# A hybrid S5/RWKV-7 block: the gated S5 projection beside the last RWKV halves, the modulation product in four column groups, a third context half early

## The chip, the core and the metric

The kernel runs on one core of a Trainium2 chip. The core has TensorE (PE, matrix products into PSUM), VectorE (DVE), ScalarE (ACT), GpSimd (POOL) and the queues that issue DMAs; they run side by side, each takes its instructions in order, and they wait for one another by semaphores. The metric is the device time of one execution in microseconds (us).

## What is computed

One layer over 256 latent tokens (with 256 context tokens as a prefix), model width 2048, in f32. Cut from the reference:

```python
mod = silu(c) @ ada_w + ada_b                  # six groups of 2048: sh1, sc1, g1, sh2, sc2, g2
z = modulate(rms_norm(h, norm1_w), sh1, sc1) @ w_in     # for context and latent tokens
y_s5 = s5_mixer(z[S5 columns])                 # complex diagonal state space, both directions
y_rw = rwkv_mixer(z_rw + (neighbour_mean(z_rw) - z_rw) * rw_mu)   # 16 heads of 64, both directions,
                                               # latent scans start from the context's final state
glu = gelu(y_s5) @ s5_glu_w                    # 1024 -> 4096
s5_out = glu[:, :2048] * sigmoid(glu[:, 2048:])
rw_out = y_rw @ rw_proj                        # 1024 -> 2048
h = x + g1 * ((gates_a * s5_out + gates_b * rw_out) @ w_o)
h = h + g2 * swiglu(modulate(rms_norm(h, norm2_w), sh2, sc2), w13, w2)
out = rms_norm(h, norm_f)
```

A step of the RWKV scan is `s = s*w - (s kk) (kk a)^T + v k^T`; the kernel works on blocks of tokens, for which it inverts small triangular matrices.

## The kernel before

The program plans itself while it is built. `Kernel.drive` holds a model of each engine's time (`Clock`) and chooses at each step between the next piece of dense work and the background generators (`spawn`); the order it finds is then the fixed order of instructions on each engine. What a thing costs on the chip plays no part once the order is written. Every operation passes through one helper and shows line 315 in the profile, so operations are told apart by the names of their tiles.

**Dense work** (`Dense`, line 353) is a list of weight halves of 128x1024 f32: first w_in (134 halves), then the modulation product (192), `glu` (32), `proj` (16), `wo` (32), w13 and w2. A half is loaded by a DMA on SP into a ring of three tiles, split by ACT into `hi` (a copy in fp32r) and by DVE into `lo` (what is left), and multiplied: each 128x128 tile takes three matmuls of 128x256, hi by xh, hi by xl, lo by xh. Each 128 output rows gather in one PSUM tile `psacc`, which an evacuation (`e_glu`, `e_proj`, ...) takes over.

**The modulation product** (groups g1, sh2, sc2: 6144 columns for one vector `sc` = silu(c)) is different ("raw" mode): no splitting, halves of 256 KB through a ring of four tiles. The vector is the stationary operand, one column of it, the weights stream: two f32 matmuls with output 1x256 a half. Sixteen K tiles accumulate one row of 256; then `e_mod` copies the row (`arow`), two transposes (`psmod`) turn it into columns and DVE adds the bias into `ada`. A record of the profile is half of an f32 matmul, so a half has four records.

**The RWKV chain** is cut into eight halves of two head pairs each: 0 to 3 context, 4 to 7 latent. For a half there are fronts (decay and rates: `pslb`, `SC`, `E`, `H`), backs (`pshg` and `psgp`, K and R products, transposes), then for two halves at once an inversion on DVE (`rw_invert`: 31 steps of `lth` and `Nh`, from `Lh` to `t11h`), two sets of 32x32 products (`pswp`, `pswq`) and the chain itself (`rw_chain`: `psxp`, `psup`, `pssp`, `psy1`, `psy2`, step after step). Latent halves end in a post-processing (`rw_post`: `psmp`, `psvp`, `psgp7`). The memory of the halves comes in slots that `rw_room` opens and closes as stages free memory.

**The stages around the change** (`body`, line 2244): beside w_in run the S5 branch and, once "room" is given, fronts and backs of halves 0 to 3. When the last half of w_in is done, inversion 0 begins, and the modulation product fills PE between the steps of halves 0 to 7. When half 7 is inverted and the product is over, the last chain (6/7) runs; after it the memory of the slots is closed, a ring for `glu` and everything later is opened (`d.open(self.n_mod, d.n)`), S5's result is loaded (`load_gl`), and GLU runs beside the posts of halves 6/7. Of GLU's 32 halves, some stand ahead of a change of memory, at which g2 (the second gates), `ma` (the merged halves written so far) and `hres` (the residual) are loaded by ACT; the rest follow it. Then proj, wo, w13, w2 and the final norm.

## Time and profile before

| | us |
|---|---|
| median of three runs | 2268.24 (2266.14 to 2268.9) |
| the profiled execution | 2264.35 |
| its span | 2262.5 |
| startup and first modulation products, to w_in's first matmul | 125.6 |
| w_in | to 786 |
| RWKV halves beside the modulation product | 786 to 1171 |
| last 32x32 products and chain 6/7 | 1171 to 1220 |
| GLU's first to last matmul | 1224.5 to 1342.0 |
| proj, wo, w13, w2, final norm | 1342 to 2262.5 |

The page says in which engine time is spent on the average; a stage that one engine bounds fills that engine's row, one that a chain of dependent steps bounds fills none. So the table by stage is the one to read, cut where a stage begins, with the granted clock of PE (1.00 is 2.4 GHz, 0.50 is 1.2 GHz). A timeline gives each instruction's start, and in brackets how long its engine had stood idle and what released it.

### The profile page before, as it was taken

How to read it: one execution, taken by the hardware profiler on the slowest of the kernel's cores; microseconds unless marked ns; L12 is line 12 of the kernel's file. 1: busy time of each engine (PE TensorE's matmuls, PEld its weight loads, DVE VectorE, ACT ScalarE, POOL GpSimd, SP SyncE). 2: the span in 40 equal slices, each digit the busy share in tenths (PEclk: the TensorE clock that was granted, in tenths of full speed). 3: DMA queues.
4: the chain of work that ended last, by engine and by line, in shares of the span. 5: the costliest groups of instructions: out<-in, count | busy, mean ns of one | idle time of the engine just before them, and what ended most of it. 6: DMA issues, size and time to landing. Idle time of an engine off the chain costs nothing.

```text
span 2262.5 us, 46694 instructions
## 1 busy us (share of the span) xinstructions
PE 2151.0 (95%) x19036; PEld 1888.8 (83%) x19036; DVE 1484.1 (66%) x2899; ACT 1100.7 (49%) x1908; POOL 150.5 (7%) x312
## 2 busy tenths in 40 slices
...
GB/s 370 336 159 196 175 210 180 129 173 216 222 229 149 154 134 138 159 165 152 127 163 53 264 199 185 183 228 229 226 228 228 227 218 183 182 183 185 181 184 131
DMA packets 155014, 431.65 MB, mean 191 GB/s; under 512 B 26256, under 2 KB 39568, under 8 KB 153904
## 3 DMA queue, kind: packets, MB, share of 16 engines
...
## 4 chain that ended last, share of the span: by engine, by line
PE 74%; DVE 8%; issue 7%; ACT 6%; DMA 4%; POOL 0%; ACTq 0%; SPq 0%; DVEq 0%; POOLq 0%
PE psacc L315 63%; PE adacc L315 2%; ACT AQh L315 1%; PE psyp L315 1%; PE psbu L315 1%; DVE lo L315 1%; DVE Nh L315 1%; DMA nk<-d_kvr 1%; DMA ad<-in_adaP_dram 1%; PE psss L315 1%; DVE lth L315 1%; PE pshg L315 1%; PE pskps L315 1%; PE pslb L315 1%; DVE SC L315 1%
## 5 line engine op out<-in xcount | busy, mean ns | idle before, releaser
L315 DVE TENSOR_TENSOR lo<-w,hi 128x1024 fp32r<-128x1024 f32 x478 | 584.7, 1224 | 406.7 <-ACT hi L315 397.0
L315 ACT ACTIVATE hi<-w 128x1024 fp32r<-128x1024 f32 x478 | 505.0, 1058 | 670.2 <-PE psacc L315 570.5
L315 PE MATMUL psacc<-h,hi 128*128 128x258 f32 x2816 | 509.7, 283 | 1.2 <-ACT hi L315 1.2
L315 PEld LDWEIGHTS psacc<-h,hi 128*128 128x128 f32 x2816 | 436.7, 189 | 1.4 <-ACT hi L315 1.4
L315 PE MATMUL psacc<-hl,hi 128*128 128x256 f32 x2144 | 407.1, 284 | 0.0
L315 PE MATMUL psacc<-h,lo 128*128 128x258 f32 x1408 | 399.0, 283 | 0.8 <-DVE lo L315 0.8
L315 PEld LDWEIGHTS psacc<-hl,hi 128*128 128x128 f32 x2144 | 331.5, 191 | 7.0 <-issue 6.9
L315 PE MATMUL psacc<-hl,lo 128*128 128x256 f32 x1072 | 302.4, 282 | 0.0
L315 PEld LDWEIGHTS psacc<-h,lo 128*128 128x128 f32 x1408 | 266.4, 189 | 1.0 <-DVE lo L315 1.0
L315 PE MATMUL psacc<-hid,hi 128*128 128x256 f32 x1408 | 253.5, 283 | 0.0
L315 PEld LDWEIGHTS psacc<-hid,hi 128*128 128x128 f32 x1408 | 219.6, 192 | 0.0
L315 PEld LDWEIGHTS psacc<-hl,lo 128*128 128x128 f32 x1072 | 204.3, 191 | 0.1
L315 PE MATMUL psacc<-w,sc 128*1 128x256 f32 x768 | 189.1, 388 | 14.4 <-DVE ada L315 5.5
L315 PE MATMUL psacc<-hid,lo 128*128 128x256 f32 x704 | 199.2, 283 | 0.0
L315 PE MATMUL psacc<-hc,hi 128*128 128x256 f32 x832 | 172.3, 288 | 0.0
L315 PEld LDWEIGHTS psacc<-w,sc 128*1 128x1 f32 x768 | 56.0, 84 | 116.5 <-DMA w<-in_adaR_dram 24.3
L315 PEld LDWEIGHTS psacc<-hid,lo 128*128 128x128 f32 x704 | 135.2, 192 | 0.0
L315 PEld LDWEIGHTS psacc<-hc,hi 128*128 128x128 f32 x832 | 127.2, 188 | 2.3 <-issue 1.4
L315 PE MATMUL psacc<-hc,lo 128*128 128x256 f32 x416 | 115.6, 278 | 0.0
L315 PE MATMUL psacc<-gl,hi 128*128 128x256 f32 x512 | 97.8, 293 | 13.6 <-ACT hi L315 9.0
L315 PE MATMUL adacc<-ad,sc 128*2 128x512 f32 x192 | 93.4, 643 | 13.3 <-ACT sc L315 7.3
L315 PEld LDWEIGHTS psacc<-gl,hi 128*128 128x128 f32 x512 | 83.7, 200 | 15.2 <-ACT hi L315 9.2
...
## 6 DMA issues: line engine op xcount, KB each, us to landing
w<-in_w_dram SPq DMA_DIRECT2D x264, 512.0 KB, 4.2
w<-in_win_dram SPq DMA_DIRECT2D x134, 512.0 KB, 4.3
w<-in_adaR_dram SPq DMA_DIRECT2D x192, 256.0 KB, 2.9
ad<-in_adaP_dram SPq DMA_DIRECT2D x48, 512.0 KB, 6.5
w<-in_glu_dram SPq DMA_DIRECT2D x32, 512.0 KB, 4.4
w<-in_wo_dram SPq DMA_DIRECT2D x32, 512.0 KB, 3.6
adg<-in_adaG_dram POOLq DMA_DIRECT2D x32, 512.0 KB, 5.6
ad<-in_adaD_dram SPq DMA_DIRECT2D x16, 512.0 KB, 7.6
```

The lines of the kernel that those rows point to most:

```text
L315: return f(*a, **k)
```

## The change

Four things, of one design.

- *Modulation product.* Its weights are laid out anew: a half has four K tiles of one block of 128 columns. `scp` holds each column of `sc` at place 15 of 31 zeros, so that a window of 16 columns puts it in row j. Four f32 matmuls a half (stationary 128x16, streaming 128x128) write to PSUM partitions 32g to 32g+16, g = 0 to 3: four column groups. 64 halves gather 16 rows in each group; then `e_mod` takes four ACT copies, four products with parts of the identity that add the groups up, and one DVE addition of 16 columns, three times in all instead of 24.
- *Third context half early.* The slot of half 2 is opened at "room", ahead of halves 0/1, so the fronts and backs of three halves, and inversion 0 and its 32x32 products, stand beside w_in.
- *GLU on a ring of its own.* `Dense` may hold two sets of rings. When half 5 is done, a ring with two buffers (`ahead=1`) for GLU is opened in freed memory, S5's result loaded, and GLU's halves follow the modulation product as fill beside halves 6 and 7 and their posts; the ring for proj and later is opened when the chains are over. Merged halves all go to memory (`d_ma`) and are loaded again after GLU; the gates' tiles share the four tiles of the modulation ring.
- *Loads of g2, ma and hres* stand after all of GLU. The planner's cost of an fp32r matmul has a floor of 0.12 us, and of the new product 0.47 of a matmul's; its spans change.

```diff
-SPANS = (None,330,100)
+SPANS = (None,280)
...
-    out["adaR"] = aw[:, 2 * D:5 * D].reshape(8, 2, P, 24, 256).transpose(3, 0, 2, 1, 4).reshape(192, P, 512)
+    out["adaR"] = aw[:, 2 * D:5 * D].reshape(4, 4, P, 48, P).transpose(3, 0, 2, 1, 4).reshape(192, P, 512)
...
             if lhs.dtype == F32R:
-                return n / 2400 + 0.002
+
+                return max(n / 2400 + 0.002, 0.12)
...
-    def open(self, first, cap, side=None):
+    def open(self, first, cap, side=None, ahead=2):
+
+        es = ExitStack()
+        if not self.rings:
+            assert not self.fifo and not self.hi
+            self.loaded = self.prepped = first
+        wr = es.enter_context(self.kern.pool("wr", bufs=ahead + 1, side=side))
+        hr = es.enter_context(self.kern.pool("hr", bufs=ahead + 1, side=side))
+        self.rings.append((first, cap, ahead, wr, hr, es))
+
+    def ring(self, i):
+        return next((r for r in self.rings if r[0] <= i < r[1]), None)
...
         if self.raw():
...
+            job, k = tiles[0]
+            if k == 0:
+                self.opened += 1
+                self.accs[job.id] = self.psd.tile([P, P], F32, tag="acc", name=f"psacc{job.id}")
+            acc = self.accs[job.id]
+            self.kern.clk.side = self.kern.clk.part = 0.47
+            for g in range(4):
+                nc.tensor.matmul(acc[32 * g:32 * g + 16], lhsT=job.rhs(k, g), rhs=self.raws[0][:, g * P:(g + 1) * P],
+                                 start=(k == 0), stop=(k == job.k - 1))
...
-        mods = [Job(16, 256, lambda k: self.sc[:, k, 0:1], lambda acc, b=b: self.e_mod(b, acc)) for b in range(24)]
+        part = lambda k, g: self.scp[:, 4 * (k % 4) + g, 15 - k // 4:31 - k // 4]
+        mods = [Job(64, P, part, lambda acc, q=q: self.e_mod(q, acc)) for q in range(3)]
         for h in range(192):
-            halves.append((A["adaR"][h], [(mods[h // 8], 2 * (h % 8) + e) for e in range(2)]))
+            halves.append((A["adaR"][h], [(mods[h // 64], h % 64)]))
...
+    def e_mod(self, q, acc):
+
+        nc = self.nc
+        yield "scalar", acc
+        ar = self.arow[:, q % 2 * P:q % 2 * P + P]
+        gs = [slice(32 * g, 32 * g + 16) for g in range(4)]
+        for g in gs:
+            nc.scalar.activation(ar[g], acc[g], AF.Copy)
+        self.dense.drop()
+        yield "tensor:1", self.arow
+        tp = self.bank([P, 16], f"psmod{q}")
+        for g in gs:
+            nc.tensor.matmul(tp, lhsT=ar, rhs=self.cs("ident")[:, g], start=(g.start == 0), stop=(g.start == 96))
+        f = 32 + 16 * q
+        yield "vector", tp
+        nc.vector.tensor_tensor(self.ada[:, f:f + 16, 0], tp, self.pc("adab", f, f + 16), op=ALU.add)
...
         yield from self.wait("room")
+        opened("s2", (2,))
         opened("sA", (0, 1))
         yield from self.wait("gates")
-        opened("sB", (2, 3), "right")
+        opened("s4", (4,), "right")
+        opened("s3", (3,), "right")
...
         self.drive(self.n_win)
+        d.open_raw(self.yp, self.n_win, self.n_mod)
...
-        self.drive(self.n_mod, early, all=False, span=SPANS[1])
...
-        d.open(self.n_mod, d.n)
+        self.drive(self.n_mod, early, all=False, span=SPANS[1],
+                   stop=lambda: ("half", 5) in self.flags)
+
+        rooms = self.slotx
+        rooms["s5"].close()
+        d.open(self.n_mod, self.n_glu, ahead=1)
         d.top_up()
+        glx = ExitStack()
+        glp = glx.enter_context(self.pool("glp"))
+        self.gates = {}
+        self.spawn(self.load_gl(glp), "gl")
+        self.drive(self.n_glu, early, all=False)
+
+        rooms["s6"].close()
+        rooms["s4"].close()
+        d.open(self.n_glu, d.n, side="right")
+        d.top_up()
...
+        with self.pool("yw", side="right") as yw:
+            late.append(self.spawn(self.load_yr(yw), "yr"))
+            self.drive(self.n_glu, late)
...
+        for k in range(0, 16, 4):
+            nc.scalar.dma_start(self.g2[:, k:k + 4], self.d_gate[1, :, k:k + 4])
+            nc.scalar.dma_start(self.ma[:, k:k + 4], self.d_ma[:, k:k + 4])
+        self.mg = [mgp.tile([P, 16, T], F32R, tag=f"mg{e}", name=f"mg{e}") for e in range(2)]
+        for k in range(0, 16, 4):
+            nc.scalar.dma_start(self.hres[:, k:k + 4], A["xT"][:, k:k + 4])
+        self.drive(self.n_proj, drain=False)
```

How instructions stand now, at three places. First VectorE at the end of w_in, around the beginning of inversion 0 (`Lh`); `lo` is a half of w_in. Before, where the last `lo` of w_in lies further up:

```order
L315 SCALAR_TENSOR_TENSOR SC_4_1_9181<-cst,SC_4_1_9181 128x256
L315 TENSOR_SCALAR AK_4_1_9182<-AK_4_1_9182,hka 128x256
L315 SCALAR_TENSOR_TENSOR AK_4_1_9182<-AK_4_1_9182,kt_4_8962 128x256
L315 TENSOR_TENSOR AK_4_1_9182<-AK_4_1_9182,kt_4_8962 128x256
L315 STREAM_TRANSPOSE Lh_9248<-dch_9192 128x1024
L315 TENSOR_TENSOR lth_0_9285<-Lh_9248,Nh_9249 128x31
L315 TENSOR_TENSOR Nh_9249<-Nh_9249,lth_0_9285 128x31
L315 SCALAR_TENSOR_TENSOR H_4_0_9328<-AK_4_0_9046,SC_4_0_9045 128x4x64
```

and now:

```order
L315 STREAM_TRANSPOSE Lh_8815<-dch_8693 128x1024
L315 TENSOR_TENSOR lth_0_8853<-Lh_8815,Nh_8816 128x31
L315 TENSOR_TENSOR Nh_8816<-Nh_8816,lth_0_8853 128x31
L315 TENSOR_TENSOR AK_5_0_8738<-AK_5_0_8738,kt_5_8656 128x256
L315 TENSOR_TENSOR lth_1_8865<-Lh_8815,Nh_8816 128x60
L315 TENSOR_TENSOR Nh_8816<-Nh_8816,lth_1_8865 128x30x2
L315 TENSOR_TENSOR lo_8872<-w_8683,hi_8856 128x1024
L315 TENSOR_TENSOR lth_2_8894<-Lh_8815,Nh_8816 128x87
```

The inversion moved ahead: thirteen halves of w_in are split (`lo`) between its steps, where none was.

Second TensorE at w_in's last matmuls (`hl` is the normed latent input), before:

```order
L315 MATMUL psacc_0_9214<-hl_178,hi_9139 128x256
L315 MATMUL psacc_0_9214<-hl_179,hi_9139 128x256
L315 MATMUL psacc_0_9214<-hl_178,lo_9161 128x256
L315 MATMUL psvt_4_9335<-cst,v_4_8965 128x128 x2
L315 MATMUL psvt_4_9335<-cst,v_4_9327 128x128 x2
L315 MATMUL pshg_4_0_0_9359<-KR0h_9319,H_4_0_9328 128x64
L315 MATMUL pshg_4_0_1_9360<-KR1h_9320,H_4_0_9328 128x64
```

and now:

```order
L315 MATMUL psacc_0_9520<-hl_179,hi_9479 128x256
L315 MATMUL psacc_0_9520<-hl_180,hi_9479 128x256
L315 MATMUL psacc_0_9520<-hl_179,lo_9491 128x256
L315 MATMUL pswqh_1_9701<-AQh_7898,w1h_9537 32x32 x32
L315 MATMUL pshg_5_1_0_9781<-KR0h_8451,H_5_1_9591 128x64
...
L315 MATMUL psacc_9799<-w_9737,scp 16x128 x4
...
L315 MATMUL psxph_0_9836<-SV0h_7617,KR0h_7612 64x64
L315 MATMUL psxph_0_9836<-SV1h_7618,KR1h_7613 64x64
```

The 32x32 products of inversion 0 (`pswq` the last of them) moved to w_in's end, and chains 0/1 (`psxp`) stand 22 rows behind it, with four halves of the modulation product (`w,scp`) ahead; before, `psxp` came 127 rows behind w_in's end.

Third TensorE inside the last chain (halves 6 and 7, `pssp` to `psy2`), before:

```order
L315 MATMUL pssph_0_13934<-SV0h_11699,HT0h_11697 64x64
L315 MATMUL pssph_0_13934<-SV1h_11700,HT1h_11698 64x64
L315 MATMUL psuph_0_13943<-xsh_0_13910,AQh_13034 64x64 x8
L315 MATMUL psy2h_0_13958<-AQh_11696,SV0h_11699 64x64
L315 MATMUL psy2h_0_13958<-AQh_11696,SV1h_11700 64x64
```

and now:

```order
L315 MATMUL pssph_0_14678<-SV0h_11930,HT0h_11928 64x64
L315 MATMUL pssph_0_14678<-SV1h_11931,HT1h_11929 64x64
L315 MATMUL psacc_0_14589<-gl_13521,hi_14474 128x256
L315 MATMUL psacc_0_14589<-gl_13522,hi_14474 128x256
L315 MATMUL psacc_0_14589<-gl_13521,lo_14477 128x256
...
L315 MATMUL pssph_0_14699<-SV0h_13330,HT0h_13328 64x64
L315 MATMUL pssph_0_14699<-SV1h_13331,HT1h_13329 64x64
```

GLU's matmuls now stand between steps of the chain.

## Rows read from the trace of the kernel before

**Rows 1.** The page, busy time of each engine: us, share of the span, instructions.

```profile
PE 2151.0 (95%) x19036; PEld 1888.8 (83%) x19036; DVE 1484.1 (66%) x2899; ACT 1100.7 (49%) x1908; POOL 150.5 (7%) x312
```

**Rows 2.** Table by stage: stretch, us, busy us (instructions) by engine, PEclk, DMA share, GB/s.

```profile
640.00:786.00 146.00, 143.61 (x1568) 133.54 (x1566) 84.17 (x144) 97.24 (x178) 20.85 (x45) 0.99 0.58 176
786.00:850.70 64.70, 55.56 (x525) 30.63 (x523) 43.17 (x120) 39.27 (x89) 4.71 (x13) 0.79 0.40 123
850.70:888.60 37.90, 34.26 (x523) 22.63 (x523) 23.18 (x58) 31.55 (x79) 10.03 (x21) 1.00 0.42 114
888.60:1005.30 116.70, 105.79 (x1154) 57.80 (x1152) 87.35 (x225) 74.72 (x180) 17.02 (x38) 0.99 0.54 159
1005.30:1138.50 133.20, 123.60 (x1446) 69.72 (x1446) 101.56 (x260) 79.20 (x180) 13.95 (x30) 0.97 0.51 154
1138.50:1171.00 32.50, 22.98 (x102) 7.40 (x100) 26.21 (x70) 3.04 (x5) 0.00 (x0) 0.98 0.59 184
1171.00:1183.60 12.60, 7.75 (x256) 7.34 (x256) 0.00 (x0) 11.13 (x16) 0.00 (x0) 0.50 0.21 49
1183.60:1219.80 36.20, 29.31 (x648) 24.97 (x648) 12.78 (x40) 18.27 (x49) 1.07 (x2) 0.96 0.12 41
1219.80:1342.00 122.20, 103.29 (x784) 100.39 (x785) 68.70 (x94) 60.48 (x90) 11.26 (x21) 0.92 0.66 212
1342.00:2262.00 920.00, 902.77 (x7494) 901.71 (x7493) 553.25 (x791) 394.24 (x478) 17.46 (x33) 0.99 0.65 198
```

**Rows 3.** Timeline of VectorE, an inversion's first and another's last instruction: start, us, instruction.

```profile
786.82 1.24 DVE L315 STREAM_TRANSPOSE Lh<-dch 128x1024 f32<-128x1024 f32 x1
...
1168.97 2.00 DVE L315 STREAM_TRANSPOSE t11h<-Nh 128x1024 f32<-128x1024 f32 x1
```

**Rows 4.** Timeline of TensorE, the sets that move: start us, us, what, count [idle before].

```profile
849.64 1.13 PE L315 MATMUL pslb<-wad,lw 64*128 64x256 f32 x4
...
929.58 1.98 PE L315 MATMUL pswph<-t11h,AQh 32*32 32x32 f32 x64
...
942.25 2.21 PE L315 MATMUL pswqh<-AQh,w1h 32*32 32x32 f32 x128
...
1178.32 3.62 PE L315 MATMUL pswqh<-AQh,w1h 32*32 32x32 f32 x126 [0.30 <-ACT w1h L315]
```

**Rows 5.** Timeline of TensorE, first steps of chains 0/1.

```profile
850.86 0.22 PE L315 MATMUL psxph<-SV0h,KR0h 128*64 128x64 f32 x1
850.87 0.22 PE L315 MATMUL psxph<-SV1h,KR1h 128*64 128x64 f32 x1
```

**Rows 6.** Table by stage of the modulation product's instructions alone (PE, PEld, ACT).

```profile
888.60:1005.30 116.70, 58.71 (x246) 17.57 (x244) 0.00 (x0) 0.99 0.54 159
1005.30:1138.50 133.20, 66.66 (x276) 20.38 (x276) 0.00 (x0) 0.97 0.51 154
```

**Rows 7.** The page, DMA issues: count, KB each, median us to landing.

```profile
w<-in_adaR_dram SPq DMA_DIRECT2D x192, 256.0 KB, 2.9
...
w<-in_glu_dram SPq DMA_DIRECT2D x32, 512.0 KB, 4.4
```

**Rows 8.** The page, costliest groups: busy, mean ns | idle before.

```profile
L315 DVE TENSOR_TENSOR lo<-w,hi 128x1024 fp32r<-128x1024 f32 x478 | 584.7, 1224 | 406.7 <-ACT hi L315 397.0
L315 ACT ACTIVATE hi<-w 128x1024 fp32r<-128x1024 f32 x478 | 505.0, 1058 | 670.2 <-PE psacc L315 570.5
```

**Rows 9.** Table of two later stretches, TensorE alone: the w13 stage.

```profile
1480.30:1992.30 512.00, 510.09 (x4228) 1.00 0.71 216
```

**Rows 10.** Timeline of ScalarE and its DMA issues within GLU.

```profile
1254.34 0.38 ACT L315 ACTIVATE glth<-psacc 128x256 f32<-128x256 f32 x1 [1.54 <-PE psacc L315]
...
1263.50 0.33 ACTq L315 DMA_DIRECT2D ma<-d_ma  x1
...
1268.72 2.95 ACT L315 ACTIVATE hi<-w 128x1024 fp32r<-128x1024 f32 x3
```

**Rows 11.** Timeline of TensorE at the same place.

```profile
1269.83 0.80 PE L315 MATMUL psacc<-gl,hi 128*128 128x256 f32 x2 [9.04 <-ACT hi L315]
```

207 lines of the change are left out of this document (92 added, 115 removed).

## The prediction

> **What bounds the kernel now.** I read the page's busy times first, then a table by stage, then single engines at the seams. TensorE (PE) is busy 95% of the span [rows 1], which hides that the middle is not bound by it. In the table [rows 2] the last stretch (GLU's end to the finish) keeps PE at 902.8 of 920.0 us, and the stretch before 786 at 143.6 of 146: dense matmuls, back to back. Between them lie 556 us of the RWKV chain, cut at the starts of the four inversions and of the chains: 64.7 + 37.9 us (w_in's end to inversion 2), 116.7 and 133.2 (to inversions 4 and 6), then 32.5 + 12.6 + 36.2 + 122.2 = 203.5 to the end of GLU. Here the order of dependent steps is the bound: an inversion holds VectorE (DVE), then 32x32 products, then a chain in which PE, ScalarE (ACT) and DVE take turns. The four inversions follow one another and each period is filled with halves of the modulation product. Two things in the table are to be seen: DVE is busy only 84 of 146 us before 786, while an inversion (786.8 to about 823, and 32.5 us for the last) needs it; and from 1138 to 1342 the tail has three stretches with an idle engine: DVE at 0.0 in 12.6 us, no modulation product in the 36.2 us of the last chain, and PE at 103.3 of 122.2 afterwards, although 768 GLU matmuls wait. [Rows 3] give the first inversion's start and the last one's end.
>
> **The sum, by stages, against the profiled run's own span of 2262.5 us.** Its time was 2264.35, so 1.85 us lie around the span; the median of the three runs is 2268.24, 3.9 above that run. I carry both over.
>
> *1. w_in gets longer, +16 us.* The third context half brings three sets of K/R products, three LoRA sets, two transposes of v, and the two pairs of 32x32 products of inversion 0 into the stretch where PE is full. A LoRA set took 1.13 us, one head pair's pswp 1.98, the two pswq together 2.21, and 3.62 at a granted clock of 0.50 [rows 4, 2]. With 1.2 us for a set of sixteen (estimate from the LoRA set): 3 x 1.2 + 3 x 1.13 + 2 x 0.6 + 2 x 1.98 + (2.21 to 3.62) = 14.4 to 15.8, rounded up for waits. DVE gets the inversion (36 us) and about 13 us of fronts: 84.2 + 49 = 133 of 162 us, full but not over. Should `lo` come late because it stands behind substitution steps, PE waits: +25. Below +8 I see no way, since PE has no gap there. w_in ends at about 802.
>
> *2. w_in's end to inversion 2, −52 us.* Of the 102.6 us the first 64.7 (inversion 0, its products, fronts) now lie before w_in's end. What remains is a set of products, four modulation halves (together about 5 us), the chain of halves 0/1 with what follows it (37.9 us) and some front work of halves 6/7 that stood beside the inversion, 7 us: 50 us. Ends: 45 and 62.
>
> *3. Inversion 2 to inversion 6, −8 us.* Before, the product's records number 246 and 276, four to a half, so 62 + 69 = 131 halves, busy 125 us of PE [rows 6], 0.95 us each. After, 153 halves stand there. Their cost I can bound from both sides. Four matmuls of 128 columns stream as many columns as two of 256, so one after another they cost 0.95 again. If the four column groups run beside each other, it is about a quarter. For overlap speaks [rows 5]: two matmuls with 64-wide outputs in different halves of the partitions start 0.01 us apart. But the weights are then the limit: a half lands in 2.9 us [rows 7] through a ring of four tiles, so 0.73 us per half in a run of many, and inside the inversions runs of 8 to 15 halves stand. 153 x 0.73 = 112 us, against 125; 13 us saved, of which I take 8, since DVE (87.4 and 101.6 us busy) holds part of that time anyway. Removing 24 ACT copies, 48 transposes and 24 DVE additions, for 12 copies, 12 products and 3 additions, helps the same way and is in the 8. Low end: the first period took 101.8 us with 39 halves, so with free halves the two periods could go to 203.6, −46; half of it, −25, is my end. High end: +15, all 153 at 0.95 on the path and no help.
>
> The Trainium skill, "TensorE: Matmul & The Clock Gate", Part 3 ("Measured speedup vs the span model"), gives 2.38 times for three column tiles; that would make an estimate of 0.35 us for a half and, by itself, put stage 3 near its low end. The trace of before has no such matmul with 16-wide outputs to test it.
>
> *4. Inversion 6 to GLU's end, 203.5 to 167, −36 us.* After, 18 modulation halves and 228 of the 768 GLU matmuls stand beside inversion 6, 54 beside the 32x32 products, 60 inside the last chain, 72 among its post-processing, 354 after it. A matmul of this form takes 512.0 / 4228 = 0.121 us [rows 9], so the five parts are 27.6, 6.5, 7.3, 8.7 and 43 us. Inversion: 32.5 us alone, plus some ten `lo` and gate operations on DVE, 42 us (PE: 18 x 0.73 + 27.6 = 41, level with it). Products: 12.6 plus part of the fill, 18. Chain: 36.2 alone with PE 29.3 busy, plus 7.3 of fill of which most finds a gap, plus ACT's `hi` in its queue, 41. Posts: 9 of fill plus steps, 16; they took from 1219.8 to 1249 before, when GLU's first weights and gl arrived only then. The rest: 43 us at full rate, but this ring has two buffers, and a half needs 4.4 us to land [rows 7] plus 1.06 for `hi` and 1.22 for `lo` [rows 8]: 6.7 / 2 = 3.3 us per half against 2.9 of PE, 50 us at worst; 47. Sum 42 + 18 + 41 + 16 + 47 = 164, with 3 for seams 167. Ends: −50 and −15.
>
> *5. A stop at the start of proj, +7 us.* The gates' second half, the merged halves and the residual are now loaded by twelve DMA issues on ACT, behind GLU's last tanh. The same series before: from the tanh at 1254.34 the first `ma` issue came at 1263.50 and the next `hi` at 1268.72 [rows 10], and PE stood 9.04 us [rows 11]. That stop lay inside the 203.5 and is gone there. Now three halves (8.7 us of PE) are ready as cover: 13.8 of ACT plus `hi` 1.06 and `lo` 1.22 less 8.7 is 7. Ends 5 and 16 (a wait for all of GLU's writes). From there 920 us are instruction for instruction as before.
>
> Span: 802 + 50 + 242 + 167 + 7 + 920.5 = 2188.5; the run 2190; the median of runs, with the 3.9, **2194 us**.
>
> **Rivals.** *The column groups don't overlap.* Then 153 halves cost 0.95 each, 145 us instead of 112, and stage 3 comes to +16, stage 4 loses 4: 2222. For it: nothing before writes 16-wide outputs. Against: [rows 5].
>
> *GLU is fed one half at a time.* `hi` and `lo` stand in order behind chain steps that wait for PE, and two buffers leave little slack. At 6.7 us for each of the 22.5 halves behind inversion 6, 151 us stand against 122 in my sum: +29, 2223. Against: before, GLU kept PE at 103.3 of 122.2 us among the same post-processing, with the 9-us stop in it [rows 2, 11]; but there it had three buffers.
>
> *The modulation product becomes cheap*, 0.3 us a half, when the ring refills during chain steps: stage 3 at −40, 2162.
>
> *Slower: TensorE at the lower clock through the chains.* When PE worked little, the granted clock fell: 0.50 in 1171 to 1183.6, 0.79 in 786 to 850.7 [rows 2]; the pswq pair took 3.62 us there instead of 2.21 [rows 4]. The new product gives PE fewer busy microseconds between inversions. A chain has about 28 us of PE work; four chains at 1.2 instead of 2.4 GHz would add 4 x 28 = 112 us and give about 2305. It decides the sign where the mean clock in the chains falls below 0.6: 112 x (1/0.6 − 1) = 75, all of the gain. Against: the last chain, with no dense matmul in it at all, ran at 0.96 [rows 2].
>
> By the Trainium skill, "TensorE: Matmul & The Clock Gate", Part 1 (the clock gate), a PE that has gone idle runs at 1.2 GHz until it has been busy again; this speaks against thinning the fill, and the 0.50 stretch agrees while the 0.96 one shows that chain steps alone can be enough.
>
> **How the numbers follow.** My forecast with its neighbourhood (2170 to 2212) gets 0.60, cheap modulation 0.10, the first two rivals or a mix of them (2212 to 2250) 0.20, the slow clock or a w_in stretched by starving 0.07 slower, 0.03 for the same time. Two runs of this kernel can be told apart from about 0.2%. The terms' ends, added as independent errors (9, 9, 20, 18 and 5 us), make some ±30 us; the upper end goes on to the two smaller-gain rivals: 2165 to 2238. Faster 0.90, same 0.03, slower 0.07.
>
> **What would show it.** Step 1: the last hl matmul at 795 to 810, and DVE over 80% before it. Step 2: psxp of halves 0/1 within 6 us of w_in's end, inversion 2 at about 852. Step 3: four w,scp records starting together and runs of halves at 0.7 to 0.8 us each with PE waiting for their DMA; inversion 6 near 1094. Step 4: gl matmuls between the steps of the last chain, GLU over at about 1261. Step 5: PE idle 5 to 16 us some 9 us into proj, ended by `hi`. Wrong would be: w,scp records in file (first rival), gl waits of 3 us on `hi` after `hi` (second), a clock under 0.7 in the chains (last), or proj to the end longer than 920 us.

## The result: faster by 1.5%, under half of the forecast gain

The changed kernel takes 2233.96 us in the median of 4 runs (2230.21 to 2238.72) against 2268.32 for the kernel before (4 runs beside it): a ratio of 0.9851, 95% interval 0.9831 to 0.9871. The sign held, and the time lies at the upper end of the range of 2165 to 2238; the gain is 34 us where 74 were forecast. That the range held is luck in part: 12.8 us of the gain come from stages that the prediction took to be unchanged, and without them the time would be about 2247. The profiled run of the changed kernel is its slowest of the four, 2238.72 us with a span of 2236.9, so the stages below add up to 25.6 us and not to 34. Runs of one program differ by up to 18 us (2212.4 to 2229.99 in e6 below), and w_in ends between 823.3 and 833.8 us in kernels with the same order up to there, the profile of after being the latest of them. So I read differences of stages below some 5 us from single profiles, and of w_in below some 10, as nothing, unless several kernels show them.

The page after has less work on TensorE (2151.0 us in [rows 1]) and as much on the others:

```profile
PE 2093.1 (94%) x19780; PEld 1889.1 (84%) x19780; DVE 1472.3 (66%) x2879; ACT 1103.1 (49%) x1897; POOL 156.6 (7%) x325
```

Table by stage of the kernel after, same columns as [rows 2] (stretch, us, busy us (instructions) of PE, PEld, DVE, ACT, POOL, granted clock, DMA share, GB/s). Cuts: 126 (end of the start), inversion 0's begin, w_in's end, begin of inversions 2, 4 and 6, end of inversion 6, begin and end of the last chain, GLU's end, proj's end, finish:

```profile
126.00:771.20 645.20, 629.24 (x5484) 607.09 (x5484) 481.43 (x1089) 340.80 (x683) 69.75 (x141) 0.98 0.55 173
771.20:833.80 62.60, 59.24 (x637) 57.33 (x636) 52.50 (x113) 37.77 (x61) 4.42 (x10) 0.96 0.46 142
833.80:896.30 62.50, 51.85 (x899) 37.46 (x900) 32.51 (x81) 48.87 (x124) 11.35 (x26) 0.83 0.52 163
896.30:1004.10 107.80, 85.46 (x1410) 55.49 (x1410) 84.78 (x213) 67.32 (x159) 16.98 (x38) 0.75 0.62 190
1004.10:1154.60 150.50, 118.02 (x1848) 76.28 (x1848) 103.38 (x255) 84.27 (x184) 10.93 (x24) 0.69 0.57 183
1154.60:1190.60 36.00, 32.20 (x250) 28.99 (x250) 33.27 (x80) 11.95 (x20) 4.90 (x9) 0.79 0.50 159
1190.60:1215.80 25.20, 23.48 (x457) 22.09 (x458) 8.59 (x10) 22.25 (x38) 2.15 (x4) 0.93 0.40 128
1215.80:1243.70 27.90, 27.45 (x573) 24.44 (x573) 15.39 (x43) 16.75 (x41) 2.62 (x5) 1.00 0.22 69
1243.70:1314.40 70.70, 62.27 (x465) 58.97 (x466) 41.21 (x58) 37.22 (x53) 9.74 (x19) 0.95 0.53 171
1314.40:1375.20 60.80, 49.76 (x387) 48.85 (x386) 37.37 (x64) 22.71 (x33) 2.15 (x4) 0.89 0.81 286
1375.20:2236.90 861.70, 844.24 (x7111) 843.16 (x7109) 512.56 (x729) 375.19 (x445) 15.94 (x30) 0.99 0.64 200
```

Against the steps of the sum, in us:

| step | before | after | forecast | measured |
|---|---|---|---|---|
| 1 start to w_in's end | 785.7 | 833.8 | +16 | +48 |
| 2 w_in's end to inversion 2 | 102.9 | 62.5 | −52 | −40 |
| 3 inversion 2 to 4, 4 to 6 | 116.7 + 133.3 | 107.8 + 150.6 | −8 | +8 |
| 4 inversion 6 to GLU's end | 203.4 | 159.8 | −36 | −44 |
| 5 proj | 46.1 | 60.8 | +7 | +15 |
| 6 wo, w13, w2, finish | 874.5 | 861.7 | 0 | −13 |

Steps 1 and 3 lost most of the gain, steps 2 and 5 some more; steps 4 and 6 were better than forecast. In the table of after the clock column is new: 0.83, 0.75 and 0.69 from w_in's end to inversion 6, where [rows 2] had 0.79 to 1.00.

### The profile page after: what moved, and what is told of

It reads as the page before. It is cut to its first block, busy times and chain, and to the rows that moved or that the text cites. A ratio compares the mean times of both kernels' runs of the same rounds, so it can differ in the third digit from the quotient of the medians.

```text
span 2236.9 us, 48212 instructions
## 1 busy us (share of the span) xinstructions
PE 2093.1 (94%) x19780; PEld 1889.1 (84%) x19780; DVE 1472.3 (66%) x2879; ACT 1103.1 (49%) x1897; POOL 156.6 (7%) x325
## 4 chain that ended last, share of the span: by engine, by line
PE 68%; DVE 10%; ACT 9%; DMA 9%; issue 3%; POOL 0%; SPq 0%; ACTq 0%; DVEq 0%; POOLq 0%
PE psacc L315 56%; DMA w<-in_adaR_dram 4%; DVE lo L315 3%; PE adacc L315 2%; ACT hi L315 1%; PE psyp L315 1%; PE psbu L315 1%; ACT AQh L315 1%; ACT L315 1%; DMA w<-in_glu_dram 1%; PE psss L315 1%; DMA ad<-in_adaP_dram 1%; DMA nk<-d_kvr 1%; DMA d_win<-win 1%; ACT SV1h L315 1%
## 5 line engine op out<-in xcount | busy, mean ns | idle before, releaser
L315 PE MATMUL psacc<-hl,hi 128*128 128x256 f32 x2144 | 416.5, 288 | 0.0
L315 PEld LDWEIGHTS psacc<-hl,hi 128*128 128x128 f32 x2144 | 336.9, 193 | 7.8 <-issue 7.2
L315 PE MATMUL psacc<-hid,hi 128*128 128x256 f32 x1408 | 239.4, 276 | 0.0
L315 PEld LDWEIGHTS psacc<-hid,hi 128*128 128x128 f32 x1408 | 211.8, 188 | 0.0
L315 PE MATMUL psacc<-hid,lo 128*128 128x256 f32 x704 | 194.3, 276 | 0.0
L315 PE MATMUL psacc<-w,scp 128*16 128x128 f32 x1536 | 96.5, 362 | 53.5 <-DMA w<-in_adaR_dram 52.1
L315 PEld LDWEIGHTS psacc<-w,scp 128*16 128x16 f32 x1536 | 33.3, 107 | 107.9 <-DMA w<-in_adaR_dram 97.4
L315 PE MATMUL psacc<-mg,hi 128*128 128x256 f32 x512 | 90.5, 279 | 0.0
```

Source lines behind the costliest of these rows:

```text
L315: return f(*a, **k)
```

## The experiments

Times are medians of 4 runs (10 for e8, e9 and e11, one for e12), beside the kernel before on the same chip; a stage time is from the one profiled run. "After" is the changed kernel, and "the tail" the stage from inversion 6 to GLU's end.

**One part alone, or one part taken out.** First the new modulation product in the kernel before, without the other parts.

> The kernel before with the new modulation product alone (four column groups, e_mod three times), nothing else of the change. Theory R (the ring of four weight tiles sets the pace, about 1.07 us a half in runs, as PE's 49 us of waits for these weights in the changed kernel say): the product no longer costs PE 0.95 us a half, but inversions are filled at the ring's pace and PE idles at the lower clock; time between 2255 and 2275. Rival M (the new product itself brings the gain the prediction gave it): 2235 to 2250. Rival N (the product in column groups is what hurts periods 4 to 6): over 2280.

```diff
-                nc.tensor.matmul(acc, lhsT=job.rhs(k), rhs=self.raws[0][:, c * job.n:(c + 1) * job.n], start=(k == 0), stop=(k == 15))
+            for g in range(4):
+                nc.tensor.matmul(acc[32 * g:32 * g + 16], lhsT=job.rhs(k, g), rhs=self.raws[0][:, g * P:(g + 1) * P],
+                                 start=(k == 0), stop=(k == job.k - 1))
...
+        mods = [Job(64, P, part, lambda acc, q=q: self.e_mod(q, acc)) for q in range(3)]
```

Measured 2270.61 us, ratio 1.0019 (1.0004 to 1.0035): the product alone brings nothing, as theory R expected. The two periods between inversions 2 and 6 take 125.5 + 132.4 = 257.9 us (before 250), though PE is busy only 98.1 and 99.3 us in them (before 105.8 and 123.6), at a clock of 0.70 and 0.78.

Then the reverse, the changed kernel with the old product:

> The changed kernel with the old modulation product (two matmuls of 256 columns with a stationary of one column, 24 rows turned by transposes). Theory V (the new product saves PE time that the ring of four weight tiles gives back as waits, 49 us of them; e1 showed no gain from it alone): within 8 us of 2234. Rival U (beside GLU's fill the PE time saved counts): 15 to 35 us slower, 2249 to 2269.

```diff
-        mods = [Job(64, P, part, lambda acc, q=q: self.e_mod(q, acc)) for q in range(3)]
+        mods = [Job(16, 256, lambda k: self.sc[:, k, 0:1], lambda acc, b=b: self.e_mod(b, acc)) for b in range(24)]
```

Measured 2258.74 us, 0.9969 (0.9955 to 0.9982): 25 us slower than after, as rival U had it. The periods between inversions 2 and 6 take 107.0 and 148.3 us, in sum 3 less than in after; the difference lies in the tail, 191.9 us instead of 159.8. The table by stage of this product's matmuls alone in that kernel, from inversion 2 to 4, to 6, and to GLU's end (us, busy us and matmuls, clock, DMA share, GB/s), shows why:

```profile
884.80:991.90 107.10, 51.42 (x213) 0.95 0.49 154
991.90:1140.10 148.20, 75.23 (x300) 0.97 0.54 169
1140.10:1332.00 191.90, 38.16 (x160) 0.97 0.52 164
```

40 halves (160 / 4) are left behind inversion 6 and GLU comes after them; with the new product 6 are left (48 matmuls at eight to a half). The next run keeps the new product and takes out GLU's fill:

> The changed kernel in which GLU's matmuls may not start before chain 6/7 and its posts are done; rings, loads and everything else as in the changed kernel. The prediction's term 4 says that GLU beside halves 6 and 7 is worth 36 us: from inversion 6 to GLU's end 190 to 205 us instead of 160, time 2262 to 2280. If the fill slows inversion and chain by what it brings, less than 15 us are lost, under 2249.

```diff
-        self.drive(self.n_glu, early, all=False)
+        self.drive(self.n_mod, early, all=False)
```

2259.86 us, 0.9971 (0.9958 to 0.9983), and a tail of 189.1 us, both just below the ranges expected. So the fast product without GLU's fill, or the fill's ring without the fast product, leaves the tail at about 190; only both give 160. The two gains are one and the same 25 us, which needs both.

The context half:

> The changed kernel, but the slot of context half 2 is announced only when w_in is done, as in the kernel before; inversion 0 still stands beside w_in. Theory A (w_in's extra 48 us are the moved work, pauses of about 3 us in which PE waits for ACT, and the lower clock behind each pause): without the third half w_in ends 8 to 16 us earlier, at 813 to 822 in the profile, and inversion 2 comes later behind w_in by as much or more; time 2230 to 2250. Rival I (inversion 0 on DVE starves `lo` and is what stretches w_in): w_in still ends at 827 or later.

```diff
-                self.flags[("slot", g)] = 0.0
+                if g != 2:
+                    self.flags[("slot", g)] = 0.0
...
         yield from self.wait("gates")
+        self.flags[("slot", 2)] = 0.0
```

2238.16 us, 0.9874 (0.9853 to 0.9895): the third half is worth some 4 us, within the ranges of the runs. It moved 25 us out of w_in's end to inversion 2 (87.6 without it, 62.5 with it), cost w_in 9 to 20 (814.1 against 823.3 to 833.8), and the tail is 23 shorter without it (136.4 and 159.8), with 103 GLU matmuls ahead of inversion 6. All this is as theory A expected; that ACT makes the pauses, this run doesn't test.

The floor in the planner's cost, which sets no instruction but only their order, alone in the kernel before, and taken out of after:

> The kernel before with one line of the planner changed (the cost of an fp32r matmul at least 0.12 us, as in the changed kernel), so only the order of instructions differs. Theory A says nothing hangs on it: within 5 us of 2266. Rival P (the new plan itself, not what is moved, makes part of the loss in w_in): w_in ends 5 us or more behind 785.7 and the time is over 2272.

```diff
-                return n / 2400 + 0.002
+                return max(n / 2400 + 0.002, 0.12)
```

2251.05 us, 0.9936 (0.9921 to 0.9951). Inversion 0 begins at 752.6 us in this kernel, beside w_in, where before it began at 786.82 [rows 3]; w_in ends 16.7 us later and inversion 2 still begins 6.5 us earlier. So neither expectation held: w_in does end later, as rival P had it, and yet the kernel is faster. The order alone gives 0.64%, some 15 us, over two fifths of what the whole change gives.

> The changed kernel with the planner's old cost of an fp32r matmul (no floor of 0.12 us); only the order of instructions changes. Theory F (the floor is what lets the plan put inversion 0 beside w_in; alone it made the kernel before 0.64% faster): inversion 0 begins at w_in's end or later, w_in ends before 815, inversion 2 comes 80 us or more behind it, time 2240 to 2255. Rival G (the third half's early slot does that by itself): the time stays within 6 us of 2234.

```diff
-                return max(n / 2400 + 0.002, 0.12)
+                return n / 2400 + 0.002
```

2233.03 us, 0.9854 (0.984 to 0.9869), the same as after: theory F was right about the order and wrong about the time. Here inversion 0 stays behind w_in (at 801.2 us), and w_in ends at 797.9. The tables from 126 us to w_in's end, of before, of this kernel and of after (columns as above), part step 1 into its pieces:

```profile
126.00:785.70 659.70, 654.89 (x5836) 636.76 (x5834) 498.09 (x1091) 350.51 (x684) 72.08 (x143) 1.00 0.59 182
```

```profile
126.00:797.90 671.90, 664.16 (x5861) 644.91 (x5860) 497.31 (x1096) 354.96 (x696) 69.01 (x136) 1.00 0.54 177
```

```profile
126.00:833.80 707.80, 688.48 (x6119) 664.41 (x6119) 533.92 (x1201) 378.57 (x743) 74.16 (x151) 0.98 0.54 170
```

Read so, the third half costs 12.2 us, and the inversion beside w_in the other 36: PE's idle time goes from 7.7 to 19.3 us, its busy time from 664 to 688. The floor changes the whole order, so this is the price of the plan that has the inversion there, not of the inversion's own steps: of the 19.3 us, 16.0 lie ahead of its first instruction (645.20 less 629.24 in the first row of the table of after), among the fronts and backs that now have to be ready sooner. How much of the busy time is the clock shows e6 (below), which has the same order up to w_in's end and as much idle time, but is busy 10 us less:

```profile
126.00:823.70 697.70, 678.27 (x6104) 656.33 (x6103) 533.59 (x1199) 378.61 (x742) 72.01 (x145) 0.99 0.53 172
```

So of the 36 us some 12 are waits and 10 a lower clock that another run didn't have; the other 14, the moved products and what e6 itself lost by the clock, stay undivided. What the plan saves behind w_in (107.5 to 62.5) covers the 36 us and 9 more, and those are paid back: periods and tail sum to 403.3 us here, with 103 GLU matmuls ahead of inversion 6, and to 418.2 in after.

**What sets the middle.** The first idea was that the weights' ring lets too few transfers fly.

> The changed kernel with three modulation weight tiles in flight instead of four. Theory R: landing 3.4 us and about 0.9 us of use and reissue over three tiles is 1.43 us a half instead of 1.07; of the 192 halves some 110 stand in runs, so +25 to +45 us, 2260 to 2280. Rival T (the DMA engines' throughput is the limit, not the number in flight): no change, within 6 us of the changed kernel's 2234.

```diff
-        while len(self.raws) < self.RAW and self.raw_next < self.raw_to:
+        while len(self.raws) < 3 and self.raw_next < self.raw_to:
```

2222.1 us, 0.9815 (0.979 to 0.984): 12 us faster than after, which neither theory had. As three tiles are no slower than four, the ring's depth is no limit. In inversion 2, 36 halves are issued in 40.2 us with three tiles and 34 in 40.2 with four; all transfers together move 249 and 243 GB/s there. The planner knows the number of tiles, so the order changes too: inversion 2 to 4 takes longer (121.2 us), the tail less (145.1), with no half left behind inversion 6 and some 20 GLU matmuls ahead of it.

> The changed kernel with half of each modulation weight half loaded (128 KB for 256 KB) and the two column groups that lack theirs fed from the loaded part; the order of instructions is the same. The modulation vectors are not the reference's, all else is computed. Theory R and rival T both expect a faster feed: 0.7 to 0.9 us a half instead of 1.07, 2210 to 2225. If the weights' feed is not what holds inversions 2 to 6, the time stays within 6 us of 2234.

```diff
-            self.nc.sync.dma_start(t, self.halves[self.raw_next][0])
+            self.nc.sync.dma_start(t[:, 0:256], src[:, 0:256])
...
-                nc.tensor.matmul(acc[32 * g:32 * g + 16], lhsT=job.rhs(k, g), rhs=self.raws[0][:, g * P:(g + 1) * P],
+                nc.tensor.matmul(acc[32 * g:32 * g + 16], lhsT=job.rhs(k, g), rhs=self.raws[0][:, g % 2 * P:(g % 2 + 1) * P],
```

2217.38 us, 0.9788 (0.9766 to 0.981), within the expected range, though not by the expected pace (35 halves are issued in the 37.5 us of inversion 2's substitution, 1.07 us each). A half lands in 2.2 us instead of 3.4; inversion 4 to 6 takes 140.8 us instead of 150.6, PE's waits for weights there 16.8 instead of 27.7. The bytes do matter, for about 10 of the 17 us that this period lost.

> The changed kernel; each of the 768 modulation matmuls is followed by one with a stationary of zeros on the same weights and the same PSUM rows, which adds nothing to the sum and keeps PE twice as busy in the inversions (0.82 us a half, still under the feed's 1.07). Theory K (part of the loss in inversions and the 32x32 products is the clock, 0.57 to 0.63 there): clock near 1.0 from 896 to 1150 us, 8 to 25 us faster, 2209 to 2226. Rival R alone: the feed is the whole loss, no change or up to 8 us slower.

```diff
+                for z in range(1):
+                    nc.tensor.matmul(acc[32 * g:32 * g + 16], lhsT=self.kern.zz, rhs=rhs, start=False, stop=last and z == 0)
```

2239.43 us, 0.9882 (0.9861 to 0.9903). The granted clock of the two periods (columns as above) comes back to 0.91 and 0.88, and they take 114.4 and 154.4 us, not less than at 0.75 and 0.69, so theory K's gain did not come:

```profile
890.30:1004.70 114.40, 92.71 (x1960) 68.66 (x1952) 84.89 (x212) 67.36 (x159) 16.98 (x38) 0.91 0.58 180
1004.70:1159.10 154.40, 124.17 (x2600) 94.11 (x2600) 103.69 (x256) 84.96 (x184) 11.67 (x24) 0.88 0.58 184
```

That alone doesn't clear the clock: product and zeros hold PE for 108.0 us in the two periods, where the product alone held it for 78.6, so the periods could have grown by 29 us and grew by 10.5. A gain of up to some 19 us could hide there. The trace of e3 says more. From inversion 4 to its chain, the substitution and the steps behind it, the same instructions run at a clock as low as in after:

```profile
995.75:1033.37 37.62, 29.64 (x354) 16.34 (x356) 33.98 (x97) 8.73 (x25) 2.25 (x5) 0.55 0.48 141
1033.37:1058.27 24.90, 24.70 (x540) 18.78 (x540) 9.20 (x19) 21.42 (x41) 2.13 (x4) 0.58 0.40 121
```

These 62.5 us are 72.3 in after (clock 0.58 and 0.54) and 61.1 in before (1.00 and 0.87). So what this stretch lost against before goes with the bytes of the weights and not with the clock. Whether a higher clock would win something beyond that stays open, as PE is busy in 24.70 of the last 24.90 us.

Next, in-order queues. On SP's queue the loads of the S5 result stand among the modulation weights and wait for VectorE.

> The changed kernel with one edit: the eight loads of the S5 result (bvl from d_y) are issued by POOL instead of SP. Theory Q (they wait for VectorE in SP's in-order queue and hold the modulation weights behind them, so PE stands and inversion 6 comes late): inversion 4 to inversion 6 falls from 150.6 to 135 to 142 us, PE's wait for weights in that period from 27.7 to under 20 us, the kernel from 2234 to 2219 to 2228. Rival D (the halves' landing time and the extra steps on VectorE set it, the queue's order doesn't): 147 to 153 us there, the kernel within 2229 to 2239.

```diff
-                nc.sync.dma_start(raws[k].rearrange("p (t c) -> p t c", c=64), src[k])
+                nc.gpsimd.dma_start(raws[k].rearrange("p (t c) -> p t c", c=64), src[k])
```

2231.2 us, 0.9845 (0.9825 to 0.9865); inversion 4 to 6 takes 148.7 us, PE's waits for weights 25.9. The result loads in SP's queue were not it, and this theory fell. GLU's first four weight loads stand in the same queue and were not moved; in after no modulation load is issued from 1102.6 to 1115.4 us, and PE's longest wait for weights, 5.27 us, ends at 1120.57. VectorE, which prepares inversion 6, has no wait from 1108 to 1121 us, so this one doesn't reach it directly. To find the place I cut the period from inversion 4 to 6 at four landmarks: the end of the substitution (`t11h`), the first and the last addition of `pssp` to the chain's state `S`, and the next inversion:

| inversion 4 to 6, us | substitution | to the chain | chain | to inversion 6 |
|---|---|---|---|---|
| before | 34.8 | 26.4 | 35.5 | 36.6 |
| after | 41.9 | 30.3 | 31.2 | 47.1 |
| old product (e9) | 36.7 | 26.8 | 38.6 | 46.3 |
| half the bytes (e3) | 37.6 | 24.9 | 31.2 | 47.1 |

The first column goes with the product and its bytes, the last with neither. In the substitution of inversion 4, the tables of before and after:

```profile
1005.20:1040.00 34.80, 31.42 (x176) 12.58 (x174) 33.13 (x99) 7.40 (x22) 1.17 (x3) 1.00 0.76 231
```

```profile
1004.00:1045.90 41.90, 29.81 (x356) 15.21 (x354) 33.92 (x96) 8.79 (x25) 2.25 (x5) 0.58 0.75 239
```

VectorE's work is nearly the same (33.13 and 33.92 us); 6.3 of the 7 us are waits. In the list of waits of the same stretch in after, PE for the weights and VectorE for PE and ACT (us in total, times, longest):

```profile
PE psacc L315 <- DMA w<-in_adaR_dram: 11.8, 14, 1.7
```

```profile
DVE KR0h L315 <- PE psgp L315: 2.0, 2, 1.8
DVE SC L315 <- ACT SC L315: 1.9, 1, 1.9
DVE ada L315 <- PE psmod L315: 1.9, 1, 1.9
```

In before, PE waited 1.1 us for weights there, and the list has no wait of VectorE. The front's products (`psgp`) stand in PE's queue behind halves whose weights haven't landed; VectorE's front steps wait for them, and the substitution stands behind these on the same engine. The planner takes 0.73 us for a half's transfer. With the rate that the trace shows:

> The changed kernel, with the planner's transfer rate for the modulation weights set to 240 GB/s instead of 360 (the trace shows 243 to 248 in the inversions); only the order changes. Theory S (PE stands in order behind halves that haven't landed, and the front's products and VectorE's substitution behind it): the substitutions of inversions 2 and 4 take 35 to 38 us instead of 40.3 and 41.9, PE's waits for weights between inversions 2 and 6 fall from 43.9 us to under 30, the kernel to 2216 to 2228. Rival (the waits only move, since the same bytes have to land before GLU): substitutions shorter, but more halves after inversion 6, the kernel within 2229 to 2239.

```diff
-            self.dma = max(self.dma, t0) + n / (360e3 if last >= 128 else 180e3)
+            self.dma = max(self.dma, t0) + n / ((240e3 if "adaR" in src.tensor.name else 360e3) if last >= 128 else 180e3)
```

The substitutions of inversions 2 and 4 fall to 30.1 and 36.1 us, from 40.3 and 41.9, as the mechanism has it. But PE's waits for weights between the two inversions and the sixth stay at 41.9 us (43.9), the steps from the substitution to the chain grow to 39.0 and 38.4, and from the chain to inversion 6 to 61.9, with 122 GLU matmuls already in it. 2243.25 us, 0.9902 (0.9881 to 0.9923): 9 us slower than after, outside both expected ranges. The waits move, they don't go.

The next run explains most of the last column of the table.

> The changed kernel, with the split of the S5 result (eight loads, eight steps on ScalarE, eight on VectorE) not begun before inversion 6 has its inputs. Theory G (these steps stand in the two queues ahead of inversion 6's inputs): from the last step of chains 4 and 5 to inversion 6 37 to 40 us instead of 47.1, from inversion 4 to 6 140 to 144 instead of 150.6; inversion 6 to GLU's end grows by as much or more, because GLU can start only after it: 168 to 175, the kernel 2230 to 2245. Rival: the stretch before inversion 6 stays at 45 to 48 us, since the weights of the last halves set it.

```diff
         src = self.d_y.rearrange("(k p) t c -> k p t c", p=P)
         raws = []
+        yield from self.wait(("back", 15, 0), ("back", 15, 1))
```

2225.95 us, 0.9819 (0.98 to 0.9837); from the chain to inversion 6 40.0 us instead of 47.1, inversion 4 to 6 142.1 instead of 150.6, and the tail grows by only 4 us, to 163.9, so that the kernel is faster than either side expected. VectorE's timeline ahead of inversion 6 (`Lh`) in after (start, us, instruction, in brackets the idle time before it and what ended it) shows how the split `gl` held it:

```profile
1145.09 1.82 DVE L315 COPY dch<-AQh 32x512 f32<-32x512 f32 x2
1150.90 1.13 DVE L315 TENSOR_TENSOR gl<-bvl,gl 128x256 fp32r<-128x256 f32 x2 [3.99 <-ACT gl L315]
1152.06 1.11 DVE L315 COPY dch<-AQh 32x512 f32<-32x512 f32 x2
...
1154.65 1.24 DVE L315 STREAM_TRANSPOSE Lh<-dch 128x1024 f32<-128x1024 f32 x1
```

Two of VectorE's four `dch` copies, which the inversion reads, stand behind a `gl`, which waits for the `gl` of ACT, which stands behind ACT's own `dch` copies and `pR`. From the chain's end on, `gl` and the two `lo` add 6.9 us of VectorE work, and VectorE waits another 6.7 us for ACT's `gl`; the waits cost the period as much as the work. The e18 run still has one such wait of 3.68 us, and its last part is still 3.4 us longer than in before.

**The seam at proj.**

> The changed kernel with the twelve loads of g2, ma and hres issued by POOL instead of ACT. Theory Q (ACT, blocked in its queue by these issues until 18 us after GLU's last tanh, is why proj takes 60.8 us instead of 46.1): proj takes 47 to 51 us, time 2221 to 2227. Rival D (the 6 MB have to land before proj can be evacuated, whoever issues them): proj stays at 57 us or more, time within 5 us of 2234.

```diff
-            nc.scalar.dma_start(self.g2[:, k:k + 4], self.d_gate[1, :, k:k + 4])
-            nc.scalar.dma_start(self.ma[:, k:k + 4], self.d_ma[:, k:k + 4])
+            nc.gpsimd.dma_start(self.g2[:, k:k + 4], self.d_gate[1, :, k:k + 4])
+            nc.gpsimd.dma_start(self.ma[:, k:k + 4], self.d_ma[:, k:k + 4])
```

(and `hres` in the same way.) ScalarE's timeline in after shows the loads in its queue ahead of `hi`:

```profile
1315.25 0.33 ACTq L315 DMA_DIRECT2D ma<-d_ma  x1
...
1327.90 0.33 ACTq L315 DMA_DIRECT2D ma<-d_ma  x1
1328.40 4.26 ACTq L315 DMA_DIRECT2D hres<-in_xT_dram  x4
1332.70 2.00 ACT L315 ACTIVATE hi<-w 128x1024 fp32r<-128x1024 f32 x2 [16.65 <-DMA ma<-d_ma]
```

and TensorE's, where the wait of [rows 11] has its successor:

```profile
1333.81 0.80 PE L315 MATMUL psacc<-yr,hi 128*128 128x256 f32 x2 [9.76 <-ACT hi L315]
```

On POOL's queue the list of waits of proj has instead

```profile
PE psacc L315 <- ACT hi L315: 2.7, 1, 2.7
```

and proj takes 54.3 us instead of 60.8: between the 47 to 51 of theory Q and the 57 of rival D. Before, it took 46.1; of the 14.7 us that proj lost, the queue explains 6.5. The other 8 stay with the loads on POOL. All transfers together move 414 GB/s from 1324 to 1334 us in after, and 404 and 413 in two such stretches of e6, so these loads may hold back proj's own weights; no run shows it. The kernel: 2222.67 us (2212.4 to 2229.99), 0.9821 (0.9797 to 0.9846). Proj's 6.5 us are seen in all four kernels with this edit (52.8 to 54.8 us there); the other 5 us of the median are not sure: the interval reaches into after's.

**Together.**

> The changed kernel with the twelve loads for proj issued by POOL (as in e6) and three modulation weight tiles in flight (as in e2). If the two gains add (each about 11 us): 2209 to 2215. If both are the same gain (a different plan of the middle that gives back what the queue took): 2219 to 2226, no better than either.

2219.53 us, 0.9792 (0.9772 to 0.9813): proj 54.8, tail 145.2. That is 3 us under e2 and e6 each, so the two gains hardly add.

> The changed kernel with both the eight result loads and the twelve loads for proj on POOL. By theory Q the period from inversion 4 to 6 is 135 to 142 us and proj about 54 us: 2208 to 2218. By rival D the first edit adds nothing to e6: 2219 to 2226.

2232.42 us, 0.9849 (0.9821 to 0.9877), slower than both ranges: proj 53.8, but inversion 4 to 6 151.8 and the tail 162.2, so with the S5 results on POOL as well nothing is left of e6's gain beyond run-to-run differences.

> The changed kernel with the result loads and the proj loads on POOL and three modulation weight tiles in flight. If all three add: 2200 to 2212, about 0.972 of the kernel before. If they overlap: 2215 to 2225. Proj 54 us in either case; the sign of the comparison with e15 tells whether three tiles in flight are worth anything once the queue is clear.

2226.15 us, 0.9823 (0.9801 to 0.9844): the three don't add. In e14 the edits are those of e2 and e6, in e15 those of e6 and e13, in e16 all three. The best kernel is e14, three modulation tiles in flight and proj's loads on POOL: 2219.53 us against 2233.96 and 2268.3, its interval apart from both, though not from those of e2, e6 and e18. E18's edit together with these was not tried.

**Two checks of side effects.** The change also sets a size of DMA scratch memory, a line left out of the cut diff:

> The kernel before with one allocation made smaller (4096 bytes of scratch for DMA descriptors, as in the changed kernel), so that every SBUF address moves and not one instruction. The stages behind proj took 12.9 us less in the changed kernel with the same instructions: w2 239.4 instead of 253.4, wo 90.4 instead of 92.2. Theory S (where tiles lie in SBUF sets the pitch of these matmuls, 0.113 or 0.120 us): w2 or wo at a pitch other than 0.120, time 3 to 16 us off 2266. Rival O (the pitch hangs on something else): all stages as in the kernel before, within 3 us.

```diff
-    nc = bacc.Bacc("TRN2", target_bir_lowering=False, num_devices=1)
+    nc = bacc.Bacc("TRN2", target_bir_lowering=False, num_devices=1, dynamic_dma_scratch_size=4096)
```

2265.11 us, 0.9997 (0.9984 to 1.0009), all stages as before, w2 included: rival O's side. Whether the late tiles' addresses moved, the trace doesn't show.

> The changed kernel with one unused tile of 64 bytes per partition among the constants (the tile of zeros of e4, without its matmuls): the addresses behind it move, the instructions of PE stay. Theory S (addresses set the pitch of the late stages; w2 took 239.4 us in the changed kernel, 250.6 in e4, 253.4 in the kernel before): w2 about 250 us. Rival O (what moved in e4 was the stream of PE's instructions, 768 more of them): w2 at 239.4.

```diff
+            self.zz = cpool.tile([P, 16], F32, tag="zz", name="zz")
+            nc.gpsimd.memset(self.zz, 0.0)
```

One run, 2237.85 us: w_in ends 6 us earlier than in after and the tail is 7 us shorter, but w2 takes 250.6 us instead of 239.4. The page's row for the same 1408 matmuls of w2 (busy us, mean ns | idle before), in before, after and this kernel:

```profile
L315 PE MATMUL psacc<-hid,hi 128*128 128x256 f32 x1408 | 253.5, 283 | 0.0
```

```profile
L315 PE MATMUL psacc<-hid,hi 128*128 128x256 f32 x1408 | 239.4, 276 | 0.0
```

```profile
L315 PE MATMUL psacc<-hid,hi 128*128 128x256 f32 x1408 | 250.7, 281 | 0.0
```

By the code, the unused tile shifts the tiles allocated behind it by 64 bytes; the matmuls of that stage are the same, and PE has no idle time there in any of the three.

## Why the prediction was right or wrong

**Step 1, +16 forecast, +48 measured: the step that failed most.** I priced what enters w_in as PE work and took PE to stay full beside it ("133 of 162 us, full but not over" for VectorE). The third half costs 12.2 us (e10), near my 8.2 (its K/R products, LoRA sets and transposes). The inversion and its 32x32 products come to 36 with the plan they need, not 8 (26 in e6, whose w_in ends at 823.7): PE stands idle for 19.3 us since 126 us, where it stood 4.8, and its clock falls. Most of the pauses end with tiles of ScalarE, not of VectorE. Three windows of the table of after, and the one behind the last pause (columns as above):

```profile
660.00:680.00 20.00, 19.48 (x210) 17.87 (x206) 11.24 (x25) 18.60 (x33) 3.89 (x8) 1.00 0.42 125
680.00:700.00 20.00, 18.12 (x144) 16.09 (x144) 11.16 (x17) 17.73 (x35) 1.08 (x2) 1.00 0.44 145
700.00:720.00 20.00, 16.78 (x128) 15.08 (x126) 17.10 (x30) 14.49 (x25) 4.48 (x12) 0.89 0.63 201
720.00:740.00 20.00, 20.00 (x130) 17.63 (x129) 10.26 (x21) 12.22 (x27) 2.27 (x7) 0.68 0.34 108
```

Of the waits that the list of after names for PE from 640 to 833.8 us, 8.7 us end with tiles of ACT and 3.3 with tiles of VectorE, 1.4 of these with `lo`:

```profile
PE psvt L315 <- ACT HT0h L315: 2.8, 1, 2.8
PE pswqh L315 <- ACT w1h L315: 1.7, 2, 1.3
...
PE psacc L315 <- DVE lo L315: 1.4, 2, 1.0
```

ACT is busy 18.60 and 17.73 of 20 us in two of the windows. That its load is what makes these tiles late is argued, not shown: in before, ACT was busy 17.70 us from 720 to 740, and PE stood idle for 0.44. Behind a pause the granted clock falls: 0.68 from 720 to 740, with PE busy all of the 20 us. I had named "PE waits: +25" for a late `lo`; 14.5 us of waits came, few of them on `lo`, and the clock I had not put into this step at all.

**Step 2, −52 forecast, −40 measured.** The right mechanism; 12 us are missing. The 8 us behind w_in's end ran at a clock of 0.50 and the rest of the stage at 0.88, which may be where they went; no run tests it. But steps 1 and 2 belong together, and my −36 for both turned out +8. E10, in which the inversion stays behind w_in, ends at the same time: in this plan, pulling it in beside a full w_in wins nothing, since w_in pays 36 us and the rest is paid back behind it. E7 shows that with two context halves instead of three the same overlap pays: w_in +17 us, inversion 2 nevertheless 6.5 earlier.

**Step 3, −8 forecast, +8 measured: two sub-steps failed.** First the pace of the weights. I took 2.9 us of landing time through four tiles, 0.73 us a half; the trace gives 34 halves in 40.2 us, 1.18 us each (1.12 with three tiles in flight), with PE waiting 12.5 of these us for weights, and the landing time rose to 3.4 us as soon as PE asked faster (e9, with the old product, has 2.9). A sign of it was there: the substitution of inversion 4 in the kernel before already moved 231 GB/s, and after it is 239. What sets this rate stays open, since three tiles in flight do as well as four, and proj moves 414 GB/s for 10 us in the same kernel. The product itself did what it was made for. The page's rows for it, before and after (busy us, mean ns | idle before, releaser):

```profile
L315 PE MATMUL psacc<-w,sc 128*1 128x256 f32 x768 | 189.1, 388 | 14.4 <-DVE ada L315 5.5
```

```profile
L315 PE MATMUL psacc<-w,scp 128*16 128x128 f32 x1536 | 96.5, 362 | 53.5 <-DMA w<-in_adaR_dram 52.1
```

PE's part halves, by 92.6 us; its wait grows by 39, and that wait stands in an in-order queue ahead of the front's products, so the substitution inherits it (+4.8 and +7.1 us; in e3, e9 and e17 most of it is gone again). E1 shows the whole: the product alone changes nothing. By e9 it adds 3 us in this step (258.4 with it, 255.3 without): the −8 that it was to bring failed to come, and most of the +8 stands with the old product as well. Second, I counted `load_gl` as nothing in this stage. It put 4.5 us of steps and 6.7 of waits on VectorE, and 4.7 us of steps on ScalarE, ahead of inversion 6's inputs; from the chain to inversion 6 it is +10.5 us, of which e18 wins 7.1 back.

**Step 4, −36 forecast, −44 measured: right in sum.** The parts were 36.0 for the inversion (42 forecast), 25.2 and 27.9 for products and chain (18 and 41), 70.7 for the rest (63); they miss by 6 to 13 us both ways, so the sum is better than its parts. The table of the GLU matmuls alone in the same four stretches shows the fill (us, busy us and matmuls, clock, DMA share, GB/s):

```profile
1154.60:1190.60 36.00, 27.12 (x194) 0.79 0.50 159
1190.60:1215.80 25.20, 13.35 (x89) 0.93 0.40 128
1215.80:1243.70 27.90, 9.37 (x60) 1.00 0.22 69
1243.70:1314.40 70.70, 56.89 (x425) 0.95 0.53 171
```

E11 puts the price of this fill at 26 us, e9 that of the product in the same stage at 25, and neither comes without the other. The other 13 us, from 203.4 to the 190 of both runs, were not taken apart; the stop of 9.04 us in [rows 11], which moved to proj, may be most of them.

**Step 5, +7 forecast, +15 measured: the mechanism right, the size low.** PE stands 9.76 us (7 forecast, ends 5 and 16), ended by ScalarE's `hi`, behind loads on its queue that I put at 13.8 us and that held it for 16.65. In all it is idle for 11.0 us, and busy for 49.8 where proj took 46.1, at a clock of 0.89 over the stage. E6 shows the queue as the cause of 6.5 us; the rest is open.

**Step 6, 0 forecast, −13 measured.** "Instruction for instruction as before" holds, the time doesn't: by e12, which has one run, the tiles' addresses set the pitch of w2's matmuls, the time from one to the next. Without this gain of no design, the sum by stages would be −12.8.

**The rivals.** Groups that don't overlap: no. Timeline of TensorE in inversion 4, two groups of eight records, a half each:

```profile
1007.22 0.41 PE L315 MATMUL psacc<-w,scp 128*16 128x128 f32 x8 [0.38 <-DMA w<-in_adaR_dram]
...
1010.30 0.63 PE L315 MATMUL psacc<-w,scp 128*16 128x128 f32 x8 [0.54 <-DMA w<-in_adaR_dram]
```

A half takes 0.41 us, and 0.63 where the clock is low, against 0.95 before. By the factor of 2.38 for three column tiles in the Trainium skill, "TensorE: Matmul & The Clock Gate", Part 3, the 0.95 us give an estimate of 0.40 us for a half, and not the 0.35 that I wrote. The row of 0.41 agrees with it, and what I drew from it, the low end of step 3, did not come. GLU fed one half at a time: no, the tail was 159.8. The product cheap while the ring refills: no, the fastest run of eight halves in after landed 0.88 us apart, and step 3 did not shrink. The lower clock: it came (0.75 and 0.69 where 0.99 and 0.97 stood), but not in the chains, which run at 1.00 (1076.4 to 1107.5 and 1215.8 to 1243.7 us); e4, with 0.91 and 0.88, is no faster, and e3, at a clock as low, is within 1.4 us of before in inversion 4's stretch. A price of it is seen in w_in, the 10 us between after and e6. The time that came, 2234, lies where I had put the first two rivals, and neither of them came.
